# A sum of reciprocals on one core: a new work list with paired rows, multiply-and-accumulate sums and statistics put together by POOL

## The chip, the cores and the metric

The kernel runs on one core of a Trainium2 chip. The metric is the device time of an execution in microseconds, as the median of several executions; three runs of the kernel before are at hand. The profile shows one further execution, whose span is measured from its first to its last instruction.

## What is computed

The input x holds 32 x 512 x 1024 positive float32 numbers. The output is, for each of the 32 x 512 rows, the sum of the reciprocals of its 1024 numbers:

```python
def reference(x: np.ndarray) -> np.ndarray:
    return np.sum(1.0 / x, axis=-1).astype(np.float32)
```

That is 67.11 MB to read and 65,536 bytes to write.

## The kernel before, in words

The 16,384 rows lie on 128 partitions, 128 rows on each. What the kernel calls "row r" (0 to 127) is one row of 1024 numbers on every partition, 512 KB of data. A tile `ring` holds 48 rows; row r lives in place r modulo 48, so a load can start when the row 48 earlier is done. Row 127 comes as two units of 512 numbers (units 127 and 128), all others are one unit each.

No engine divides. ACT computes the reciprocal square root of a row in place (A, L150; one instruction may cover several rows), and each row's squares are then summed in one of four ways:

- B: DVE takes bn_stats of both half rows (L181) into `stats`: count, mean and variance of even and odd elements. K (L209 to L219) later turns the statistics of a group of columns into sums, as mean squared times 256 plus the variance term, adds the four parts and adds the result into `sums`. Rows that are not of kind B have zeros in `stats`, and rows of kind B zeros in `sums`, so K runs over whole stretches of columns.
- G and T: POOL squares rows in place (L191), DVE reduces them (TENSOR_REDUCE, L197).
- Z: ACT squares the row with an accumulator output (L161), which is two instructions, the second reading the accumulator.
- Q: DVE multiplies the row with itself and accumulates (tensor_tensor_reduce, L167).

The order of the work is written out by hand in `PLAN`, a list of words. A letter names the operation, the number its first unit, `+n` how many rows it takes. `D n` loads the next n rows (L141), as one DMA, or as two where the ring wraps. `O` stores the first 118 columns of `sums` in six pieces (L132). Every engine takes its own words in the order of the list: ACT takes A and Z; DVE takes B, Q, T and K; POOL takes G; SP issues D, O and the final store. Between engines, semaphores order reads and writes of the same place in a tile. The loads and stores use eight semaphores in turn, so an issue also waits until the transfer eight issues earlier has landed.

After the list, L228 adds the two parts of the last row's sum, and the last columns are stored.

Of the kernel before, what the change touches and what calls it, by code (L numbers as in the profile page):

```python
# [7 lines left out]


@with_exitstack  # L10
def kernel(
# [5 lines left out]
    nc = tc.nc  # L17
    f32 = mybir.dt.float32
    P = 128
    D = 1024  # L20
    H = D // 2
    F = 128
    R = 48
    PIECES = (512, 512)
    DONE = 118

    PLAN = """
        D16 D14 D13 A0+4 A4+4 B0 Q1 B2 A8+4 G4+3 B3 A12+4 B8 Q9 B10 Z7 G12+3 T4+3 D10 Z15 A16+4
        B11 A20+4 B16 T12+3 D9 A24+4 G20+3 B17 B18 B19 A28+2 B24 Z23 B25 G28+2 T20+3 D9 A30+4
        B26 B27 A34+4 T28+2 B30 A38+4 B31 D9 B32 B33 A42 B34 Z37 B35 A43+4 K0+32 B36 D5 B38
        A47+4 G44+2 B39 B40 B41 Z43 B42 D6 A51+2 T44+2 Z49 B46 D4 A53+4 B47 B48 B50 D4 A57+4 B51
        B52 B54 Z53 G59 B55 D5 A61 Z60 B56 G61 B57 A62+4 B58 D3 T59 D2 T61 A66+4 G63 K32+32 B64
        B65 Z62 G69 T63 D3 A70 B66 D3 G70 B67 B68 D2 A71+4 T69 T70 D2 A75+4 B71 B72 D2 B73 D1
        A79 G75 B74 D1 A80+4 B76 B78 T75 D1 D1 Z77 D1 D1 B79 D1 D1 A84 B80 A85+4 B81 B83 B84 Z82
        B85 A89+2 B86 A91+4 B87 B88 B89 A95+4 B90 B91 B92 Z96 B93 Z97 B94 A99+4 B95 B98 K64+32
        A103 B99 A104+3 G103 B101 B102 Z100 T103 G106 A107+2 B104 B105 A109+3 G107 T106 B108  # L40
        Z110 G109 T107 A112+3 B111 T109 A115+2 B112 B113 Z116 B114 A117+2 B115 A119+2 B117
        K96+22 O0 A121 G119 B120 A122 B121 Z118 B122 A123 T119 A124 B123 A125 G124 A126 B125
        A127 A128 K118+10 G127 T124 Z126 Z128 T127
    """.split()

    Arsqrt = mybir.ActivationFunctionType.Abs_reciprocal_sqrt
    Square = mybir.ActivationFunctionType.Square
    mult = mybir.AluOpType.mult
    add = mybir.AluOpType.add
# [7 lines left out]
            name=nc.get_next_instruction_name(),  # L57
# [4 lines left out]
    )  # L62

    pool = ctx.enter_context(tc.tile_pool(name="pool", bufs=1))
    ring = pool.tile([P, R, D], f32)
    stats = pool.tile([P, F, 2, 2, 3], f32)
    part = pool.tile([P, F, 4], f32)
    total = pool.tile([P, F], f32)
    sums = pool.tile([P, F + 1], f32)
    nc.gpsimd.memset(stats, 0.0)  # L70
    nc.gpsimd.memset(sums, 0.0)  # L71

    def parse(tok):
        r, _, n = tok[1:].partition("+")
        return tok[0], int(r), int(n or 1)

    def place(u):
        k = u - (F - 1)
        if k < 0:
            return u, 0, D  # L80
        return F - 1, sum(PIECES[:k]), PIECES[k]

    def area(u, n=1):
        r, at, w = place(u)
        return ring[:, r % R : r % R + n, at : at + w]

# [35 lines left out]
    def rows(u, n=1):  # L122
        spaces = []
        for r, at, w in (place(i) for i in range(u, u + n)):
            spaces += [("row", r % R, i) for i in range(at, at + w, 128)]
        return spaces

    loaded = 0
    left = set(range(DONE))

    def store(lo, hi):
        nc.sync.dma_start(out=out_v[:, lo:hi], in_=sums[:, lo:hi])  # L132

    with tc.manual_schedule():
        for op, u, n in (parse(tok) for tok in PLAN):
            if op == "D":
                n, u = u, loaded
                while n:
                    r, at, w = place(u)
                    m = min(n, R - r % R, F - 1 - u) if u < F - 1 else 1  # L140
                    inst = nc.sync.dma_start(  # L141
                        out=area(u, m), in_=x_v[:, r : r + m, at : at + w]
                    )
                    note("SP", inst, writes=rows(u, m))
                    u, n = u + m, n - m
                loaded = u
            elif op == "A":
                while n:
                    m = min(n, R - place(u)[0] % R)
                    inst = nc.scalar.activation(  # L150
                        out=area(u, m),
                        in_=area(u, m),
                        func=Arsqrt,
                        scale=1.0 - 2.0**-17,
                    )
                    note("ACT", inst, writes=rows(u, m))
                    u, n = u + m, n - m
            elif op == "Z":
                c = u - (F - 1) if u >= F else 0
                c = F if c else u  # L160
                inst = nc.scalar.activation(  # L161
                    out=area(u), in_=area(u), func=Square, accum_out=sums[:, c : c + 1]
                )
                note("ACT", inst, writes=rows(u))
            elif op == "Q":
                row = area(u)
                inst = nc.vector.tensor_tensor_reduce(  # L167
                    out=row,
                    in0=row,
                    in1=row,  # L170
                    scale=1.0,
                    scalar=0.0,
                    op0=mult,
                    op1=add,
                    accum_out=sums[:, u : u + 1],
                )
                note("DVE", inst, writes=rows(u))
            elif op == "B":
                r, at, w = place(u)
                for h in range(0, w, H):  # L180
                    inst = nc.vector.bn_stats(  # L181
                        out=stats[:, r, (at + h) // H],
                        in_=ring[:, r % R, at + h : at + min(h + H, w)],
                    )
                    half = [("row", r % R, i) for i in range(at + h, at + min(h + H, w), 128)]
                    note("DVE", inst, reads=half)
            elif op == "G":
                while n:
                    m = min(n, R - u % R)
                    row = area(u, m)  # L190
                    inst = nc.gpsimd.tensor_tensor(out=row, in0=row, in1=row, op=mult)  # L191
                    note("POOL", inst, writes=rows(u, m))
                    u, n = u + m, n - m
            elif op == "T":
                while n:
                    m = min(n, R - u % R)
                    inst = nc.vector.tensor_reduce(  # L197
                        out=sums[:, u : u + m],
                        in_=area(u, m),
                        axis=mybir.AxisListType.X,  # L200
                        op=add,
                    )
                    note("DVE", inst, reads=rows(u, m))
                    u, n = u + m, n - m
            elif op == "K":
                mean = stats[:, u : u + n, :, :, 1].rearrange("p f h e -> p (f h e)")
                var = stats[:, u : u + n, :, :, 2].rearrange("p f h e -> p (f h e)")
                tmp = part[:, u : u + n].rearrange("p f q -> p (f q)")
                nc.vector.tensor_tensor(out=tmp, in0=mean, in1=mean, op=mult)  # L209
                nc.vector.scalar_tensor_tensor(  # L210
                    out=tmp, in0=tmp, scalar=float(H // 2), in1=var, op0=mult, op1=add
                )
                nc.vector.tensor_reduce(  # L213
                    out=total[:, u : u + n],
                    in_=part[:, u : u + n],
                    axis=mybir.AxisListType.X,
                    op=add,
                )
                nc.vector.tensor_tensor(  # L219
                    out=sums[:, u : u + n],  # L220
                    in0=sums[:, u : u + n],
                    in1=total[:, u : u + n],
                    op=add,
                )
            elif op == "O":
                for c in range(0, DONE, DONE // 6):
                    store(c, min(c + DONE // 6, DONE))
        nc.vector.tensor_tensor(  # L228
            out=sums[:, F - 1 : F],
            in0=sums[:, F - 1 : F],  # L230
            in1=sums[:, F : F + 1],
            op=add,
        )
        store(DONE, F)


# [28 lines left out]
```

## Time and profile before

| what | us |
|---|---|
| median of 3 runs (172.34 to 172.53) | 172.5 |
| the profiled execution's own time | 171.93 |
| its span | 169.82 |
| DVE busy, ACT busy, POOL busy | 136.2, 135.8, 48.7 |
| first A on ACT starts | 23.10 |
| first bn_stats on DVE starts | 26.83 |
| last instruction that writes `sums` (L228) ends | 167.36 |

The profiled execution took 2.1 us more than its span, for what lies around the first and the last instruction. In the profile, "idle before" is the time that an engine stood still ahead of an instruction, and "<-" names what ended it. DVE has no idle time of note from 43.67 us to its end; all its idle time in the waits view, 30.3 us, lies before that. POOL waits for ACT for 113.5 us in all. TensorE does nothing in this kernel. The DMA queue of the loads is busy for 93.2% of the span, measured over the 16 DMA engines.

### The profile page before, as it was taken

To read this page: it belongs to the slowest core of one execution; us is meant where nothing else is said; L and a number is where in the kernel's file an instruction comes from. 1 tells how busy PE (TensorE), PEld (TensorE's weight loads), DVE (VectorE), ACT (ScalarE), POOL (GpSimd) and SP (SyncE) were. 2 spreads that over 40 slices of the span, in tenths; PEclk is the share of its full clock that TensorE was granted. 3 is DMA by queue.
4 is the path that set the end of the run, shared out by engine and by line. 5 is a ranking of instruction groups with operands and counts; after the bars stand their busy time and mean duration, and the time that the engine had idled before them with its cause. 6 is when DMAs were issued, how large, how long until landed. Compare 5 with 4: busy or idle time off the path is not lost.

```text
span 169.8 us, 437 instructions
## 1 busy us (share of the span) xinstructions
DVE 136.2 (80%) x207; ACT 135.8 (80%) x88; POOL 48.7 (29%) x24
## 2 busy tenths in 40 slices
DVE  0000006499799999999999999999999999999993
ACT  3000059998995899999998959999999999899923
POOL 4000000859089200070052580400000177104420
DMA  6998999999998999999999999999999999999600
GB/s 247 494 401 355 479 432 432 432 432 401 439 452 376 434 439 440 443 425 434 452 434 443 417 394 437 428 423 400 450 437 408 429 423 413 419 410 410 213 0 1
DMA packets 5331, 67.20 MB, mean 396 GB/s; under 512 B 1616, under 2 KB 1616, under 8 KB 2768
## 3 DMA queue, kind: packets, MB, share of 16 engines
q1 hardware_dynamic: 5328, 67.18, 93.2%
q14 instruction: 3, 0.02, 0.0%
HBM read 67.11 MB, written 0.07 MB: 396 GB/s over the span
## 4 chain that ended last, share of the span: by engine, by line
DVE 72%; DMA 23%; ACT 2%; issue 1%; SPq 0%; DVEq 0%
DVE stats L181 53%; DMA ring<-in_x_dram 23%; DVE sums L197 15%; ACT ring L150 2%; DVE part L209 1%; DVE sums L219 1%; DVE part L210 1%; DVE total L213 1%; SPq L141 0%; DVE sums L228 0%; DVEq L228 0%; DVEq L197 0%; DVEq L219 0%
## 5 line engine op out<-in xcount | busy, mean ns | idle before, releaser
L150 ACT ACTIVATE ring<-ring 128x4096 f32<-128x4096 f32 (+4 forms) x49 | 115.8, 2419 | 27.2 <-DMA ring<-in_x_dram 27.0
L181 DVE BATCH_NORM_STATS2 stats<-ring 128x6 f32<-128x512 f32 x164 | 99.3, 680 | 30.3 <-ACT ring L150 30.3
L191 POOL TENSOR_TENSOR ring<-ring 128x1024 f32<-128x1024 f32 (+3 forms) x18 | 47.0, 2609 | 113.5 <-ACT ring L150 113.5
L197 DVE TENSOR_REDUCE sums<-ring 128x1 f32<-128x1024 f32 (+3 forms) x18 | 29.4, 1649 | 0.1
L161 ACT ACTIVATE ring<-ring 128x1024 f32<-128x1024 f32 (+1 forms) x19 | 19.4, 1021 | 3.2 <-DVE sums L219 3.2
L161 ACT ACTIVATION_READ_ACCUMULATOR ring<-ring 128x1 f32 x19 | 3.5, 186 | 0.0
L167 DVE CUSTOM_DVE_ANT_0 ring<-ring 128x1024 f32<-128x1024 f32 x2 | 2.9, 1466 | 0.0
L209 DVE TENSOR_TENSOR part<-stats 128x128 f32<-128x128 f32 (+2 forms) x5 | 2.5, 502 | 0.1
L219 DVE TENSOR_TENSOR sums<-sums,total 128x32 f32<-128x32 f32 (+2 forms) x5 | 2.2, 438 | 0.2
L55 ACT ACT_TABLE_LOAD x1 | 1.3, 1283 | 0.7 <-PEq L249 0.7
L210 DVE SCALAR_TENSOR_TENSOR part<-part,stats 128x128 f32<-128x128 f32 (+2 forms) x5 | 1.5, 300 | 0.2
L70 POOL MEMSET stats<- 128x1536 f32 x1 | 1.4, 1378 | 0.3 <-POOLq L249 0.3
L213 DVE TENSOR_REDUCE total<-part 128x32 f32<-128x128 f32 (+2 forms) x5 | 1.3, 260 | 0.2
L228 DVE TENSOR_TENSOR sums<-sums 128x1 f32<-128x1 f32 x1 | 0.2, 160 | 0.1
L71 POOL MEMSET sums<- 128x129 f32 x1 | 0.2, 208 | 0.0
L249 POOL MEMSET const-float32-0.0<- 128x1 f32 x1 | 0.1, 99 | 0.2 <-issue 0.2
L167 DVE DVE_READ_ACCUMULATOR2_ANT sums<- 128x1 f32 x2 | 0.2, 80 | 0.0
L249 POOL MEMSET const-bfloat16-1.0<- 128x1 bf16 x1 | 0.1, 103 | 0.0
L249 POOL MEMSET const-uint8-127<- 128x1 uint8 x1 | 0.1, 103 | 0.0
L249 POOL MEMSET const-float32-1.0<- 128x1 f32 x1 | 0.1, 99 | 0.0
## 6 DMA issues: line engine op xcount, KB each, us to landing
ring<-in_x_dram SPq DMA_DIRECT2D x3, 4608.0 KB, 32.6
ring<-in_x_dram SPq DMA_DIRECT2D x4, 2560.0 KB, 38.4
ring<-in_x_dram SPq DMA_DIRECT2D x1, 7168.0 KB, 38.8
ring<-in_x_dram SPq DMA_DIRECT2D x1, 6656.0 KB, 54.1
ring<-in_x_dram SPq DMA_DIRECT2D x4, 1536.0 KB, 36.5
ring<-in_x_dram SPq DMA_DIRECT2D x4, 1024.0 KB, 28.6
ring<-in_x_dram SPq DMA_DIRECT2D x7, 512.0 KB, 19.6
ring<-in_x_dram SPq DMA_DIRECT2D x1, 3072.0 KB, 36.9
```

The source lines that it names most:

```text
L55: nc.scalar.add_instruction(mybir.InstLoadActFuncSet(name=nc.get_next_instruction_name(), act_func_set_id=act_sets.index("abs_reciprocal_s ...
L70: nc.gpsimd.memset(stats, 0.0)
L150: inst = nc.scalar.activation(out=area(u, m), in_=area(u, m), func=Arsqrt, scale=1.0 - 2.0**-17,)
L161: inst = nc.scalar.activation(out=area(u), in_=area(u), func=Square, accum_out=sums[:, c : c + 1])
L167: inst = nc.vector.tensor_tensor_reduce(out=row, in0=row, in1=row, scale=1.0, scalar=0.0, op0=mult, op1=add, accum_out=sums[:, u : u + 1],)
L181: inst = nc.vector.bn_stats(out=stats[:, r, (at + h) // H], in_=ring[:, r % R, at + h : at + min(h + H, w)],)
L191: inst = nc.gpsimd.tensor_tensor(out=row, in0=row, in1=row, op=mult)
L197: inst = nc.vector.tensor_reduce(out=sums[:, u : u + m], in_=area(u, m), axis=mybir.AxisListType.X, op=add,)
L209: nc.vector.tensor_tensor(out=tmp, in0=mean, in1=mean, op=mult)
L210: nc.vector.scalar_tensor_tensor(out=tmp, in0=tmp, scalar=float(H // 2), in1=var, op0=mult, op1=add)
L213: nc.vector.tensor_reduce(out=total[:, u : u + n], in_=part[:, u : u + n], axis=mybir.AxisListType.X, op=add,)
L219: nc.vector.tensor_tensor(out=sums[:, u : u + n], in0=sums[:, u : u + n], in1=total[:, u : u + n], op=add,)
```

## The change

The list is new, and with it come new operations:

- The ring has 46 places. Row 127 comes as 640 and 384 numbers. The loads are 24 words instead of 27: D2 D9 D11 D11 D13, then D12 D10 D10 D7 D7 D7 D6 D5 D4 D3 D2 D2 D1 D2 and five D1.
- Ten rows (32, 43, 47, 61, 100, 104, 105, 108, 111, 114) are summed as pairs, by 1/a + 1/b = (a + b) / (a b), where a is the first half of the row and b the second. POOL multiplies the halves into a slot of `prod` (P), TensorE adds them into a PSUM bank by two matmuls with an identity matrix (U), ACT takes the reciprocal square root of the product, scaled, and squares it (L and E, 512 numbers each), and DVE multiplies the result with the sums in PSUM and accumulates (R, a tensor_tensor_reduce).
- There are 35 Q (two of them the pieces of row 127, the second of which starts from the first one's sum), 23 B, 36 rows of G, 20 Z, and 41 rows of T. Five T rows are squared by ACT without an accumulator (C).
- K appears twice, for columns 0 to 63 and 64 to 115, and runs on POOL as five instructions; it no longer touches `sums`. A new word M, also on POOL, adds all of these columns into `sums` at once, ahead of the store O of columns 0 to 115. Columns 116 to 127 hold no B row.
- L228 is gone.
- At the start POOL makes the identity matrix (a memset and an affine_select on 128 x 128) ahead of the memsets of `stats` and `sums`.

The diff, cut to its core:

```diff
-    R = 48
-    PIECES = (512, 512)
-    DONE = 118
+    R = 46
+    NP = 5
+    PIECES = (640, 384)
+    NR = F - sum(PIECES) // D
+    KB = (0, 64, 116)
+    S = float(2**17)
+    FIT = 1.0 - 2.0**-17
...
+        D2 D9 D11 D11 D13 A0+2 Z0 Z1 A2 A3+5 A8 Q6 G3 A9+2 Q7 C8 T3 C9 Z2 Z4 Z5 A11 A12 G10+2
+        A13 A14+7 G12+2 T8+6 D12 A21 G16+3 Z19 Z20 Z21 A22+7 U32@0 P32@0 B14 Q15 T16+2 T18 D10
...
+        Q83 Z81 G80 A85+4 T79 D1 G84 T80 D1 D1 D1 T84 A89 B85 A90+2 Q86 Z82 Q87 Z88 Q89 A92+2
+        B90 Q91 A94 B92 A95+2 Q94 A97+2 Q95 Q96 Z93 G97 U100@4 B98 A99 A101 P100@4 T97 A102 B99
+        P104@0 L100 U104@5 A103 B101 G102 L104 B103 E100 E104 R100 A106+2 P105@1 U105@6 T102
+        P108@2 R104 U108@7 L105 B106 A109 L108 Q107 K64+52 E105 E108 R105 A110 U111@0 R108 Q109
+        P111@3 A112+2 Q110 L111 Q112 E111 U114@1 P114@4 A115 R111 Q113 A116 L114 Q115 A117+2
+        Q116 E114 Q117 A119+2 R114 M0 O0 Q118 A121 Q120 Z119 Q121 A122 A123 Q122 A124 Q123 A125
+        Q124 A126 Q125 A127 A128 Q127 Z126 Q128
...
+            elif op == "P":
+                slot[u], r = b, u % R
+                inst = nc.gpsimd.tensor_tensor(
+                    out=prod[:, b], in0=ring[:, r, :H], in1=ring[:, r, H:], op=mult
+                )
...
+            elif op == "U":
+                bank[u], r = b, u % R
+                for h in range(2):
+                    inst = nc.tensor.matmul(
+                        ps[:, b],
+                        lhsT=ident,
+                        rhs=ring[:, r, h * H : (h + 1) * H],
+                        start=h == 0,
+                        stop=h == 1,
+                    )
...
+            elif op in "LE":
+                pair = prod[:, slot[u]]
                 inst = nc.scalar.activation(
+                    out=pair,
+                    in_=pair,
+                    func=Arsqrt if op == "L" else Square,
+                    scale=S * FIT if op == "L" else 1.0,
+                )
...
+            elif op == "R":
+                pair = prod[:, slot[u]]
+                inst = nc.vector.tensor_tensor_reduce(
+                    out=pair,
+                    in0=pair,
+                    in1=ps[:, bank[u]],
+                    scale=S,
+                    scalar=0.0,
+                    op0=mult,
+                    op1=add,
+                    accum_out=sums[:, u : u + 1],
+                )
...
             elif op == "K":
...
+                nc.gpsimd.tensor_tensor(out=flat, in0=mean, in1=mean, op=mult)
+                nc.gpsimd.tensor_scalar(
+                    out=flat, in0=flat, scalar1=float(H // 2), scalar2=None, op0=mult
+                )
+                nc.gpsimd.tensor_tensor(out=flat, in0=flat, in1=var, op=add)
+                nc.gpsimd.tensor_tensor(
+                    out=part[:, u : u + n, :2],
+                    in0=part[:, u : u + n, :2],
+                    in1=part[:, u : u + n, 2:],
                     op=add,
                 )
+                nc.gpsimd.tensor_tensor(
+                    out=total_b[:, u : u + n],
+                    in0=part[:, u : u + n, 0],
+                    in1=part[:, u : u + n, 1],
                     op=add,
                 )
+            elif op == "M":
+                nc.gpsimd.tensor_tensor(
+                    out=sums[:, : KB[-1]],
+                    in0=sums[:, : KB[-1]],
+                    in1=total_b[:, : KB[-1]],
+                    op=add,
+                )
...
-        nc.vector.tensor_tensor(
-            out=sums[:, F - 1 : F],
-            in0=sums[:, F - 1 : F],
-            in1=sums[:, F : F + 1],
-            op=add,
-        )
-        store(DONE, F)
+        store(KB[-1], F)
```

More of the change, by code (lines that the diff above doesn't have):

```diff
@@ L7 @@
 from concourse.hw_specs import get_activation_tables
+from concourse.masks import make_identity
 @with_exitstack
@@ L22 @@
     F = 128
-    R = 48
-    PIECES = (512, 512)
-    DONE = 118
-    PLAN = """
[L32 to L43, printed above, removed]
+    R = 46
@@ new lines @@
+    NP = 5
[4 more added lines that the diff above has]
+    FIT = 1.0 - 2.0**-17
+    PLAN = """
+        D2 D9 D11 D11 D13 A0+2 Z0 Z1 A2 A3+5 A8 Q6 G3 A9+2 Q7 C8 T3 C9 Z2 Z4 Z5 A11 A12 G10+2
+        A13 A14+7 G12+2 T8+6 D12 A21 G16+3 Z19 Z20 Z21 A22+7 U32@0 P32@0 B14 Q15 T16+2 T18 D10
+        A29 G24 A30+2 Q22 G25+3 L32 Q23 Z30 E32 T24 Z31 R32 G28+2 A33 U43@1 A34+4 P43@1 T25+5
+        D10 A38 G34+2 A39 A40 Q37 A41+2 G36 Q38 L43 A44+2 G40+2 B39 T34+3 E43 C33 Z42 G44+2 A46
+        U47@2 T33 D7 A48+2 T40+2 A50+2 G46 R43 T44+2 D7 A52 P47@2 A53 G48 T46 L47 A54+2 B49 G51
+        T48 A56 Q54 A57 G52 E47 Z50 B55 G53 U61@3 A58+3 R47 B56 P61@3 T51+3 D7 A62+3 G58 B57 L61
+        G62+3 A65 T58 D6 A66 B59 A67 E61 B65 C60 R61 C67 T60 K0+64 Z66 T62+3 D5 A68+4 T67 D4 A72
+        Q68 A73+5 B69 Q70 D3 B71 B72 D2 A78+6 G74 B75 B76 T74 B77 A84 G79 B78 Z73 D2 D1 D2 D1
+        Q83 Z81 G80 A85+4 T79 D1 G84 T80 D1 D1 D1 T84 A89 B85 A90+2 Q86 Z82 Q87 Z88 Q89 A92+2
[5 more added lines that the diff above has]
+        Q124 A126 Q125 A127 A128 Q127 Z126 Q128
@@ L64 @@
     pool = ctx.enter_context(tc.tile_pool(name="pool", bufs=1))
+    pspool = ctx.enter_context(
+        tc.tile_pool(name="pspool", bufs=1, space=bass.MemoryType.PSUM)
+    )
     ring = pool.tile([P, R, D], f32)
@@ L67 @@
     part = pool.tile([P, F, 4], f32)
-    total = pool.tile([P, F], f32)
-    sums = pool.tile([P, F + 1], f32)
+    total_b = pool.tile([P, F], f32)
+    sums = pool.tile([P, F], f32)
+    prod = pool.tile([P, NP, H], f32)
+    ident = pool.tile([P, P], f32)
+    ps = pspool.tile([P, 8, H], f32)
+    make_identity(nc, ident)
     nc.gpsimd.memset(stats, 0.0)
@@ L73, in parse @@
     def parse(tok):
-        r, _, n = tok[1:].partition("+")
-        return tok[0], int(r), int(n or 1)
+        body, _, b = tok[1:].partition("@")
+        r, _, n = body.partition("+")
+        return tok[0], int(r), int(n or 1), int(b or 0)
     def place(u):
-        k = u - (F - 1)
-        if k < 0:
+        if u < NR:
             return u, 0, D
-        return F - 1, sum(PIECES[:k]), PIECES[k]
+        at = sum(PIECES[: u - NR])
+        return NR + at // D, at % D, PIECES[u - NR]
     def area(u, n=1):
@@ L126, in rows, with half @@
         return spaces
+    def half(u, at):
+        return [("row", u % R, i) for i in range(at, at + H, 128)]
     loaded = 0
-    left = set(range(DONE))
+    summed = set()
+    slot, bank = {}, {}
     def store(lo, hi):
@@ L134 @@
     with tc.manual_schedule():
-        for op, u, n in (parse(tok) for tok in PLAN):
+        for op, u, n, b in (parse(tok) for tok in PLAN):
             if op == "D":
@@ L139 @@
                     r, at, w = place(u)
-                    m = min(n, R - r % R, F - 1 - u) if u < F - 1 else 1
+                    m = min(n, R - r % R, NR - u) if u < NR else 1
                     inst = nc.sync.dma_start(
@@ L146 @@
                 loaded = u
[L147 to L154, printed above, removed]
-                    )
-                    note("ACT", inst, writes=rows(u, m))
-                    u, n = u + m, n - m
+            elif op in "AC":
+                inst = nc.scalar.activation(
+                    out=area(u, n),
+                    in_=area(u, n),
+                    func=Arsqrt if op == "A" else Square,
+                    scale=FIT if op == "A" else 1.0,
+                )
+                note("ACT", inst, writes=rows(u, n))
@@ L158 @@
             elif op == "Z":
-                c = u - (F - 1) if u >= F else 0
-                c = F if c else u
                 inst = nc.scalar.activation(
-                    out=area(u), in_=area(u), func=Square, accum_out=sums[:, c : c + 1]
+                    out=area(u), in_=area(u), func=Square, accum_out=sums[:, u : u + 1]
                 )
                 note("ACT", inst, writes=rows(u))
+            elif op == "P":
[3 more added lines that the diff above has]
+                )
+                note("POOL", inst, rows(u), [("slot", b)])
+            elif op == "U":
[8 more added lines that the diff above has]
+                    )
+                    note("PE", inst, half(u, h * H), [("bank", b)])
+            elif op in "LE":
+                pair = prod[:, slot[u]]
+                inst = nc.scalar.activation(
+                    out=pair,
[3 more added lines that the diff above has]
+                )
+                note("ACT", inst, writes=[("slot", slot[u])])
+            elif op == "R":
[10 more added lines that the diff above has]
+                )
+                note("DVE", inst, [("bank", bank[u])], [("slot", slot[u])])
@@ L165 @@
             elif op == "Q":
-                row = area(u)
+                row, r = area(u), place(u)[0]
+                total = sums[:, r : r + 1]
                 inst = nc.vector.tensor_tensor_reduce(
@@ L171 @@
                     scale=1.0,
-                    scalar=0.0,
+                    scalar=total if r in summed else 0.0,
                     op0=mult,
                     op1=add,
-                    accum_out=sums[:, u : u + 1],
+                    accum_out=total,
                 )
+                summed.add(r)
                 note("DVE", inst, writes=rows(u))
             elif op == "B":
-                r, at, w = place(u)
-                for h in range(0, w, H):
+                for h in range(2):
                     inst = nc.vector.bn_stats(
-                        out=stats[:, r, (at + h) // H],
-                        in_=ring[:, r % R, at + h : at + min(h + H, w)],
-                    )
-                    half = [("row", r % R, i) for i in range(at + h, at + min(h + H, w), 128)]
-                    note("DVE", inst, reads=half)
+                        out=stats[:, u, h], in_=ring[:, u % R, h * H : (h + 1) * H]
+                    )
+                    note("DVE", inst, reads=half(u, h * H))
             elif op == "G":
[L188 to L193, printed above, removed]
-            elif op == "T":
[L195 to L200, printed above, removed]
-                        op=add,
-                    )
-                    note("DVE", inst, reads=rows(u, m))
-                    u, n = u + m, n - m
+                row = area(u, n)
+                inst = nc.gpsimd.tensor_tensor(out=row, in0=row, in1=row, op=mult)
+                note("POOL", inst, writes=rows(u, n))
+            elif op == "T":
+                inst = nc.vector.tensor_reduce(
+                    out=sums[:, u : u + n],
+                    in_=area(u, n),
+                    axis=mybir.AxisListType.X,
+                    op=add,
+                )
+                note("DVE", inst, reads=rows(u, n))
             elif op == "K":
@@ L207 @@
                 var = stats[:, u : u + n, :, :, 2].rearrange("p f h e -> p (f h e)")
[L208 to L211, printed above, removed]
-                )
[L213 to L216, printed above, removed]
+                flat = part[:, u : u + n].rearrange("p f q -> p (f q)")
+                nc.gpsimd.tensor_tensor(out=flat, in0=mean, in1=mean, op=mult)
+                nc.gpsimd.tensor_scalar(
+                    out=flat, in0=flat, scalar1=float(H // 2), scalar2=None, op0=mult
+                )
+                nc.gpsimd.tensor_tensor(out=flat, in0=flat, in1=var, op=add)
[3 more added lines that the diff above has]
+                    in1=part[:, u : u + n, 2:],
                     op=add,
                 )
[L219 to L222, printed above, removed]
+                nc.gpsimd.tensor_tensor(
+                    out=total_b[:, u : u + n],
+                    in0=part[:, u : u + n, 0],
+                    in1=part[:, u : u + n, 1],
+                    op=add,
+                )
+            elif op == "M":
[3 more added lines that the diff above has]
+                    in1=total_b[:, : KB[-1]],
                     op=add,
@@ L225 @@
             elif op == "O":
-                for c in range(0, DONE, DONE // 6):
-                    store(c, min(c + DONE // 6, DONE))
-        nc.vector.tensor_tensor(
-            out=sums[:, F - 1 : F],
-            in0=sums[:, F - 1 : F],
-            in1=sums[:, F : F + 1],
-            op=add,
-        )
-        store(DONE, F)
+                for c in range(0, KB[-1], 20):
+                    store(c, min(c + 20, KB[-1]))
+        store(KB[-1], F)
 _INS = ['x']
```

## The prediction

> **What bounds the kernel now.** I read the page first (engine totals and the chain that ended last), then the waits, then the timeline of the first 60 us and of the last 15.
>
> ```profile
> span 169.8 us, 437 instructions
> ...
> DVE 136.2 (80%) x207; ACT 135.8 (80%) x88; POOL 48.7 (29%) x24
> ...
> DVE 72%; DMA 23%; ACT 2%; issue 1%; SPq 0%; DVEq 0%
> ```
> ```profile
> DVE stats L181 <- ACT ring L150: 30.3, 3, 26.8
> ACT ring L150 <- DMA ring<-in_x_dram: 27.0, 6, 21.1
> ```
>
> Two engines are busy for 80% each, and the chain is DVE for 72% of the span: no engine is short of hours, but DVE begins late and then never stops. ACT waits 21.1 us for the 16 rows of the first transfer, DVE 26.8 us for ACT's first group.
>
> ```profile
> 23.10 14.14 ACT L150 ACTIVATE ring<-ring 128x4096 f32<-128x4096 f32 x4 [21.08 <-DMA ring<-in_x_dram]
> ...
> 40.02 12.43 ACT L150 ACTIVATE ring<-ring 128x4096 f32<-128x4096 f32 x4 [0.71 <-DMA ring<-in_x_dram]
> ...
> 55.76 11.58 ACT L150 ACTIVATE ring<-ring 128x4096 f32<-128x4096 f32 x4 [2.27 <-DMA ring<-in_x_dram]
> ```
>
> These three waits end when the first (16 rows), second (14) and third (13) transfer land. 16.9 / 14 and 15.7 / 13 both give 1.21 us a row; 23.1 - 16 x 1.21 = 3.7, so the first n rows are there at 3.7 + 1.21 n. All 128 could be there at 158.6. The issues of L141 say when they are:
>
> ```profile
> L141 SPq DMA_DIRECT2D ring<-in_x_dram x29: 327/328/945, 0.7 to 152.4; - x29
> ...
> DMA to landing us min/median/max: 9.0/30.9/59.7
> ```
>
> The last of 29 loads is issued at 152.4 and takes at least 9.0: it lands at about 161.4, 2.8 later than the bare rate. But work goes on until 167.4:
>
> ```profile
> 164.29 0.21 DVE L209 TENSOR_TENSOR part<-stats 128x40 f32<-128x40 f32 x1
> ...
> 165.28 1.06 ACT L161 ACTIVATE ring<-ring 128x1024 f32<-128x1024 f32 x1 [3.15 <-DVE sums L219]
> ...
> 167.20 0.16 DVE L228 TENSOR_TENSOR sums<-sums 128x1 f32<-128x1 f32 x1
> ```
>
> So DVE is 6 us behind the data, and even ACT's Z126 waits 3.15 for it, because the last K adds into the same columns of sums. After 167.36 come 2.46 us of store and end (span 169.82).
>
> **DVE's work after.** From the timeline, start to start: bn_stats 0.594 a half row, TENSOR_REDUCE 1.07 a row + 0.05, multiply-and-accumulate (Q, L167) 28.03 to 29.16 = 1.13 a row. The new list has 23 B rows (27.3), 41 T rows in 23 instructions (45.0), 33 full Q rows and two pieces (37.3 + 1.2), ten R, each taken as half a Q plus its accumulator read, 0.6 (6.0): 116.8 against 136.2. The five K (7.5 us: 2.5 + 1.5 + 1.3 + 2.2) and L228 leave DVE altogether.
>
> **ACT's work after.** Four 4-row A take 14.14, and a 1-row A is followed 0.95 later (87.32 to 88.27): 0.853 a row + 0.10 an instruction. 118 rows in 65 instructions are 107.2; 20 Z at 1.04 (37.15 to 38.19) 20.8; five C at 0.95 4.8; 20 L and E on 512 elements at 0.52 (the 0.61 row less the overlap) 10.4. Sum 143.2, against 133.4 for the old list by the same rows. ACT becomes the fuller engine.
>
> **Start.** Two rows land at 6.2, A0+2, Z0 and Z1 take 3.9 (to 10.1), then ACT idles to 17.0, when rows 2 to 10 are there. From there 139.3 us of ACT work fit before 160. Up to row 109 I count nothing for ACT and DVE but the wait for data. Identity and both memsets run on POOL ahead of Z0 at 8.1; the old memsets end at 2.26, identity's two instructions are between 0.2 (L71, 129 elements) and 2 x 1.04 (L191 with 512 elements): covered by 5.8 us, and by 6.9 more of ACT's idling. Ring rows: 46 instead of 48 means that each load waits for rows 2 earlier; rows 46 to 57 need T8+6, which the sums above put near 45, while the loads already queued last until 59.4. A cover of about 14 us; gone, each microsecond past it delays all later rows by one.
>
> **POOL's work after.** L191 is 1.71 a row + 0.18: 36 G rows in 24 instructions 65.9, ten P 10.4 (512 elements, 1.04). K64 is five instructions on 208, 208, 208, 104 and 52 elements, 0.54 + 0.35 + 0.54 + 0.36 + 0.28 = 2.1 by L191's slope (bounds: five times 0.2 and five times 1.04); K0 2.3. With M and the start about 84, against 48.7. POOL is half idle, so only its place matters: K64 stands ahead of P111 and P114, on which L111, L114 wait.
>
> **The tail, which sets the end.** The new list has 24 loads; five fewer of 29 take the 2.8 us of excess to 2.3: last landing 160.9. Three paths then end together.
> - Data: A128 (0.43), Z126 (1.04 + its read 0.19): 162.6.
> - ACT: rows 110 to 113 land near 142.5 (3.7 + 114 x 1.21 = 141.6, with half the excess). From A110 on: 15 rows in 12 instructions 14.0, two pieces 1.1, Z119 and Z126 2.1, four L and E 2.1, 19.3 in all: 161.8.
> - DVE: from 143.5 (A110 done), 14 Q rows 15.8, pieces 1.2, R111 and R114 1.2: 161.7; Q128 after A128 ends at 161.9.
>
> So the last write of sums is at 162.6, and I add 0.5 for handoffs between engines (0.1 from A's end to POOL or DVE at the starts, some five in a row): 163.1. The K of the end, Z126's wait and L228 are gone: M on POOL covers columns below 116 only, and its store's six issues go out before. The final store waits for no load still under way. 163.1 + 2.46 = **165.6 span**. The profiled execution took 171.93 for a span of 169.82; 165.6 + 2.1 = 167.7, and the median of the runs is 0.57 above that execution: **168.3**.
>
> **The shared port.** Two-input DVE instructions stretch while POOL runs:
>
> ```profile
> 135.01 1.95 POOL L191 TENSOR_TENSOR ring<-ring 128x1024 f32<-128x1024 f32 x1 [24.92 <-ACT ring L150]
> ```
> ```profile
> 135.56 1.45 DVE L219 TENSOR_TENSOR sums<-sums,total 128x32 f32<-128x32 f32 x1
> ```
>
> L219 takes 0.19 elsewhere; here it ends at 137.01, just behind POOL's 136.96. The Q at 34.97 (1.72 against 1.21) and L209 at 94.78 (1.09) end just behind POOL too, while bn_stats and TENSOR_REDUCE keep their times. The list now has 35 Q instead of 2, and no row shows POOL starting during a Q. The Trainium skill (SBUF — State Buffer, Who interferes with whom) says that whichever starts first holds the port for its whole instruction and the other blocks, for DVE instructions with two SBUF inputs against POOL instructions that read SBUF. By that rule each P or K instruction could also lose up to one Q, 1.13, and R, whose second input is in PSUM, nothing.
>
> **Rivals.**
> 1. Waits on POOL in the tail. Half of 35 Q meeting POOL and waiting 1.3 on average would be 22 us; DVE has 143 us (19 to 162) for 117 of work, so 26 to spare, and until row 109 it costs little. Behind that K64, P111, P114 and M (4.5 together) stand among back-to-back Q, and ACT has 0.8 to spare for L111 and L114. Half of the 4.5, 2.3 to 2.4, lost: 170.7. The same holds if K64 costs its upper bound (5.2 - 2.1 - 0.8 = 2.3). For it: the three rows. Against: the order leaves POOL free behind P114, where eleven Q stand.
> 2. Slower: TensorE. No row of before has a matmul. Between nothing and twice the slowest row on 512 elements (2 x 1.04 = 2.1); I take 1.04, the row itself. Single pairs up to row 61 have over 10 us between landing and R. But rows 99 to 104 land near 131.5, and from there twelve matmuls (100, 104, 105, 108, 111, 114) come in one line. R108 needs eight of them; behind it DVE has 18.8 us of work (14 Q, pieces, three R), so it must start at 143.1 for 161.9. That holds up to 1.45 us a matmul; each 0.1 above costs 0.8. The median of before is passed from 2.0; at 2.2 it is 131.5 + 17.6 - 143.1 = 6.0 late: 174.3. The Trainium skill (FP8 and Floating Point Precision, TensorE Precision Notes) gives a true fp32 product four passes, and TensorE: Matmul & The Clock Gate (Part 1) 427 ns for 512 columns cold and 216 warm. By these an estimate is 1.7 us cold and 0.86 warm, that is 2.0 us late (170.3) if the array stays cold and nothing if it warms in the line.
> 3. Loads end early: were the excess of 2.8 all due to the small loads of the end, it might fall by 2 more: with ACT and DVE at 161.8 only 0.8 comes of it, unless those sums are high too; 166.4.
> 4. The list does less than it says: DVE still the bound. 116.8 + 3.5 + 26.8 would not reach 150, so only through rival 1; no more than 0.02 is left for no difference.
>
> **How the numbers follow.** Forecast 168.3, own range 166.8 to 169.8: 0.62. Rival 1: 0.19 (169.8 to 172). Rival 2 past 172.8: 0.11. Rival 3: 0.06. No difference: 0.02. The range 166.2 to 171.6 leaves out rival 2, a little of 1 and half of 3. A measurement can tell about 0.2%. Faster 0.62 + 0.18 + 0.06 = 0.86, same 0.02, slower 0.12 (a hundredth from rival 1).
>
> **What would show it.** After: ACT's first A near 6.2, 7 us of idling ahead of the second transfer, the last load landed near 161, DVE near 117 busy, ACT near 145, the last write of sums within 2.5 of the last landing. Q far above 1.21 or POOL instructions above L191's times mean the port. Wrong if R waits for PE in the last 35 us, if ACT waits for POOL over 1 us there, or if SP waits on ring rows so long that the loads run dry.

## The result, and the profile after

The changed kernel takes 178.16 us (median of four runs, 177.93 to 178.27) against 172.42 us for the kernel before on the same chip: a ratio of 1.0334, with a 95% interval of 1.0316 to 1.0352. It is slower by 5.7 us, where 168.3 us was forecast. The profiled execution took 177.93 us, with a span of 175.8.

The page of the changed kernel, engine totals and the chain that ended last:

```profile
span 175.8 us, 543 instructions
...
PE 27.6 (16%) x40; PEld 9.6 (5%) x40; DVE 135.6 (77%) x159; ACT 145.4 (83%) x131; POOL 99.2 (56%) x53
...
ACT 42%; DMA 23%; POOL 20%; DVE 8%; another core or an unknown queue 2%; issue 2%; SPq 1%; DVEq 0%
```

DVE is busy for 135.6 us, almost what it was (136.2), though the list leaves it 116.8 us of work by the rows of before. POOL has 99.2 where 84 were counted. The chain, which was DVE with some DMA, now passes through ACT, POOL and DVE.

The beginning is as forecast (timeline of ACT; start, duration, and in brackets the idle time before):

```profile
5.46 1.91 ACT L170 ACTIVATE ring<-ring 128x2048 f32<-128x2048 f32 x1 [3.46 <-DMA ring<-in_x_dram]
...
16.34 10.05 ACT L170 ACTIVATE ring<-ring 128x1024 f32<-128x1024 f32 x6 [6.69 <-DMA ring<-in_x_dram]
```

The end is not. The loads are done by 160 us (no data moves from 160 to 165), and yet work goes on for 13 us. The timeline of the last 30 us shows why:

```profile
148.21 1.45 POOL L258 TENSOR_TENSOR part<-stats 128x208 f32<-128x208 f32 x1 [5.29 <-DVE stats L238]
...
153.53 1.14 POOL L269 TENSOR_TENSOR total_b<-part 128x52 f32<-128x52 f32 x1
154.63 2.48 POOL L184 TENSOR_TENSOR prod<-ring 128x512 f32<-128x512 f32 x2
155.92 1.29 ACT L201 ACTIVATE prod<-prod 128x512 f32<-128x512 f32 x2 [8.31 <-POOL prod L184]
...
172.44 0.62 DVE L224 CUSTOM_DVE_ANT_0 ring<-ring,sums 128x384 f32<-128x384 f32 x1
```

Read from the bottom: the last multiply-and-accumulate ends at 173.06. ACT stood still for 8.31 us until POOL had multiplied the pair of row 111 (P111, L184). POOL could not do that earlier, since K64 (L258 to L269) stands ahead of it in POOL's queue, and K64 waited 5.29 us for DVE's statistics of row 106. Then it took 6.5 us (148.21 to 154.67) instead of the 2.1 of the prediction. So DVE was late by row 106, though it stood still only at the start, ahead of T8+6 and T25+5 (which starts at 61.97), and behind K64. Its waits, all of them (total, times, longest):

```profile
DVE ring L224 <- ACT ring L170: 21.9, 1, 21.9
DVE sums L247 <- POOL ring L244: 12.6, 2, 10.9
DVE prod L210 <- ACT prod L201: 2.7, 1, 2.7
```

What made it late stands in the durations, not in the waits (groups of instructions, shapes apart; busy us, mean ns):

```profile
L224 DVE CUSTOM_DVE_ANT_0 ring<-ring 128x1024 f32<-128x1024 f32 x33 | 56.4, 1743 | 22.0 <-ACT ring L170 21.9
...
L244 POOL TENSOR_TENSOR ring<-ring 128x1024 f32<-128x1024 f32 x15 | 31.3, 2102 | 41.8 <-ACT ring L170 41.7
```

A Q takes 1.74 us on average instead of 1.21: 33 x 0.53 = 17.6 us, nearly all that DVE is busy beyond the 116.8. A 1-row G takes 2.10 instead of 1.89. If the shared port is the cause, wait and work are one number in these rows; the experiments test it.

### The profile page after: what moved, and what is told of

The parts are those of the page before. It is cut to its first block, busy times and chain, and to the rows that moved or that the text cites. A ratio compares the mean times of both kernels' runs of the same rounds, so it can differ in the third digit from the quotient of the medians.

```text
span 175.8 us, 543 instructions
## 1 busy us (share of the span) xinstructions
PE 27.6 (16%) x40; PEld 9.6 (5%) x40; DVE 135.6 (77%) x159; ACT 145.4 (83%) x131; POOL 99.2 (56%) x53
## 4 chain that ended last, share of the span: by engine, by line
ACT 42%; DMA 23%; POOL 20%; DVE 8%; another core or an unknown queue 2%; issue 2%; SPq 1%; DVEq 0%
ACT ring L170 34%; DMA ring<-in_x_dram 23%; POOL ring L244 12%; DVE ring L224 5%; ACT ring L178 5%; POOL prod L184 5%; ACT prod L201 3%; DVE stats L238 1%; DVE prod L210 1%; POOL part L262 1%; POOL part L258 1%; POOL part L263 1%; SPq L163 1%; POOL total_b L269 1%
## 5 line engine op out<-in xcount | busy, mean ns | idle before, releaser
L170 ACT ACTIVATE ring<-ring 128x1024 f32<-128x1024 f32 (+6 forms) x70 | 113.8, 1687 | 15.3 <-DMA ring<-in_x_dram 15.3
L244 POOL TENSOR_TENSOR ring<-ring 128x1024 f32<-128x1024 f32 (+2 forms) x24 | 72.5, 3040 | 49.9 <-ACT ring L170 49.8
L224 DVE CUSTOM_DVE_ANT_0 ring<-ring 128x1024 f32<-128x1024 f32 (+1 forms) x34 | 57.1, 1716 | 22.0 <-ACT ring L170 21.9
L247 DVE TENSOR_REDUCE sums<-ring 128x1 f32<-128x1024 f32 (+4 forms) x23 | 46.3, 2040 | 12.6 <-POOL ring L244 12.6
L191 PE MATMUL ps<-ring,ident 128*128 128x512 f32 x40 | 27.6, 837 | 120.3 <-DMA ring<-in_x_dram 120.3
L238 DVE BATCH_NORM_STATS2 stats<-ring 128x6 f32<-128x512 f32 x46 | 28.7, 675 | 0.0
L201 ACT ACTIVATE prod<-prod 128x512 f32<-128x512 f32 x20 | 12.0, 618 | 11.0 <-POOL prod L184 11.0
L178 ACT ACTIVATE ring<-ring 128x1024 f32<-128x1024 f32 x20 | 20.8, 1041 | 0.1
L191 PEld LDWEIGHTS ps<-ring,ident 128*128 128x128 f32 x40 | 9.6, 261 | 137.4 <-DMA ring<-in_x_dram 85.3
L184 POOL TENSOR_TENSOR prod<-ring 128x512 f32<-128x512 f32 x10 | 14.5, 1462 | 0.0
L258 POOL TENSOR_TENSOR part<-stats 128x256 f32<-128x256 f32 (+1 forms) x2 | 2.1, 1042 | 8.1 <-DVE stats L238 8.1
L269 POOL TENSOR_TENSOR total_b<-part 128x64 f32<-128x64 f32 (+1 forms) x2 | 1.4, 720 | 0.2
```

The lines of the kernel that those rows point to most:

```text
L170: inst = nc.scalar.activation(out=area(u, n), in_=area(u, n), func=Arsqrt if op == "A" else Square, scale=FIT if op == "A" else 1.0,)
L178: inst = nc.scalar.activation(out=area(u), in_=area(u), func=Square, accum_out=sums[:, u : u + 1])
L184: inst = nc.gpsimd.tensor_tensor(out=prod[:, b], in0=ring[:, r, :H], in1=ring[:, r, H:], op=mult)
L191: inst = nc.tensor.matmul(ps[:, b], lhsT=ident, rhs=ring[:, r, h * H : (h + 1) * H], start=h == 0, stop=h == 1,)
L201: inst = nc.scalar.activation(out=pair, in_=pair, func=Arsqrt if op == "L" else Square, scale=S * FIT if op == "L" else 1.0,)
L224: inst = nc.vector.tensor_tensor_reduce(out=row, in0=row, in1=row, scale=1.0, scalar=total if r in summed else 0.0, op0=mult, op1=add, acc ...
```

## The experiments

Two theories stood at the start. **A**: Q and POOL hold each other up at the port, DVE has no time to spare for it, and K64's place passes the delay on. **B**: the place of K64 alone does it.

The kernel before was run again beside each group of four experiments, with medians of 172.12, 171.95 and 171.98 us, against 172.42 beside the changed kernel. So a difference between two kernels of different groups is good to about half a microsecond; each ratio is to the kernel before of its own group.

**K64 behind the pairs.** One word moves.

```diff
-        ... B106 A109 L108 Q107 K64+52 E105 E108 ... E114 Q117 A119+2 R114 M0 O0 ...
+        ... B106 A109 L108 Q107 E105 E108 ... E114 Q117 A119+2 R114 K64+52 M0 O0 ...
```

> The changed list with one word moved: K64+52 (the POOL statistics of columns 64 to 115) stands behind all pairs, just ahead of M, instead of ahead of P111 and P114. Theory A (the shared port: in the changed kernel 33 full Q took 1.74 us each instead of 1.21, so DVE is some 6 us late by row 106, and K64's place passes that on to ACT, which waits 8.3 us for P111): ACT's wait at L111 goes, but DVE stays late. From B106's end (148.1) DVE still has 15 Q, two pieces and four R, 20.9 us, so the last write of sums stays near 169 to 171, and the time is 174 to 176. Theory B (the place of K64 alone; DVE's lateness is covered): the end follows the last load, and the time is 168 to 170.

Measured: 175.31 us, ratio to before 1.019 (1.0175 to 1.0205). The waits of ACT for POOL at L201 fall from 11.0 to 3.1 us in all, the longest from 8.3 to 1.1. DVE stays late and ends at 170.2. The place of K64 is worth 2.9 us as long as DVE is late; theory B, which expected 168 to 170, falls.

**The Q of rows below 106 as B.** Eighteen words change their letter: Q6, Q7, Q15, Q22, Q23, Q37, Q38, Q54, Q68, Q70, Q83, Q86, Q87, Q89, Q91, Q94, Q95, Q96.

```diff
-        ... A8 Q6 G3 A9+2 Q7 ... Q94 A97+2 Q95 Q96 Z93 G97 ...
+        ... A8 B6 G3 A9+2 B7 ... B94 A97+2 B95 B96 Z93 G97 ...
```

> The changed list with the 18 Q of rows below 106 turned into B in the same places (two bn_stats of one SBUF input each, 1.19 us, instead of one multiply-and-accumulate with two, 1.13), K64 where it was. Theory A: no wait at the port before row 106, so DVE is some 12 us lighter and no longer late, POOL's instructions take L191's times of before again, K64 starts near 142 instead of 148.2, ACT's wait at L111 falls from 8.3 to under 2, and the time is 167 to 170. Theory B: Q's waits at the port were spare time of DVE, K64 still starts near 147 and the time stays at 176 to 178.

Measured: 170.62 us, ratio 0.9919 (0.9903 to 0.9936): 7.5 us less than the changed kernel, with the same rows and slightly dearer DVE instructions. Its groups show that both sides get their times back, and its timeline that K64 starts 7.3 us earlier:

```profile
L244 POOL TENSOR_TENSOR ring<-ring 128x1024 f32<-128x1024 f32 x15 | 28.2, 1892 | 47.3 <-ACT ring L170 47.3
...
L224 DVE CUSTOM_DVE_ANT_0 ring<-ring 128x1024 f32<-128x1024 f32 x15 | 18.5, 1286 | 0.1
```
```profile
140.95 1.45 POOL L258 TENSOR_TENSOR part<-stats 128x208 f32<-128x208 f32 x1 [0.97 <-DVE stats L238]
...
148.68 1.29 ACT L201 ACTIVATE prod<-prod 128x512 f32<-128x512 f32 x2 [3.51 <-POOL prod L184]
```

ACT still waits 3.51 us for P111, since K64 is as long as before (it stands among Q107 to Q112, which stayed), so the time is a little above the 167 to 170 that theory A expected; theory B expected 176 to 178.

**The pairs undone.** The words P, U, L, E and R of the ten pair rows go; L becomes A and R becomes B, and K64 stands ahead of M.

```diff
-        ... U111@0 R108 Q109 P111@3 A112+2 Q110 L111 Q112 E111 U114@1 P114@4 A115 R111 ...
+        ... B108 Q109 A112+2 Q110 A111 Q112 A115 B111 ...
```

> The changed list with the ten pair rows taken as A and B (no P, U, L, E, R), K64 just ahead of M since row 114 is then a B row. ACT then waits for no other engine. Theory A: DVE gains ten B of 1.19 for ten R of 0.61, 5.8 us more, less about 3 of port waits at P; it is late all the same and sets the end: 175 to 178. Theory B (ACT's stall behind POOL is the cause): 168 to 170.

Measured: 179.89 us, ratio 1.0455 (1.0438 to 1.0472). This is 1.9 us above the 175 to 178 of theory A, and far from the 168 to 170 of theory B. ACT waits for nothing but data, and the kernel is slower still: the chain is DVE for 60%, and DVE's last Q ends at 175.0. Against the list with K64 late (175.31) the ten pairs save 4.6 us, where the expectation had about 3 net. They are no fault of the change.

**The early start alone.** The kernel before, with its first loads cut smaller.

```diff
-        D16 D14 D13 A0+4 A4+4 B0 Q1 B2 ...
+        D4 D8 D8 D10 D13 A0+4 A4+4 B0 Q1 B2 ...
```

> The kernel before with only its first three loads cut otherwise (4, 8, 8, 10 and 13 rows instead of 16, 14 and 13). The early start alone: ACT's first A at 8.5 instead of 23.1, DVE some 14 us earlier. DVE has 136 us of work and was 6 us behind the last load, so if the start is worth what the prediction took it for, the end moves by 3 to 5 us and the time is 167.5 to 169.5. If the early rows only mean waiting later (rows 20 to 42 land when they did), the time stays within 1 us of 172.5.

Measured: 170.50 us, ratio 0.9908 (0.9893 to 0.9923): 1.6 us, between the two expectations. From its page and its waits:

```profile
DMA 63%; ACT 23%; DVE 8%; another core or an unknown queue 3%; SPq 1%; issue 0%; DVEq 0%
```
```profile
DVE stats L181 <- ACT ring L150: 27.3, 5, 11.9
```

DVE waits almost as long as before (27.3 against 30.3 us), only in five pieces: it starts at 11.9 and then has to wait for the rows of later loads. The chain is DMA for 63% of the span, and DVE from 152.2 us on: this list follows the data, and its last write of `sums` (to 166.4) comes some 5 us behind the last load.

**Both edits.** The eighteen Q as B, and K64 behind the pairs (the two diffs above together).

> The changed list with both edits: the 18 Q of rows below 106 as B, and K64 behind the pairs. If the time of the changed kernel is the port before row 106 plus K64's place, ACT's remaining wait of 3.5 us at L111 and DVE's 2.7 at R111 go, and the last write of sums comes 2 to 3.5 earlier than with the Q turned into B alone: 167 to 168.6. If K64's place only mattered while DVE was late, nothing is left to gain: 170 to 171.

Measured: 168.67 us, ratio 0.9812 (0.9798 to 0.9827), at the upper end of the 167 to 168.6 expected. ACT waits for no other engine any more. ACT's last instruction and DVE's, and the group of the 15 full Q that are left:

```profile
161.24 0.19 ACT L178 ACTIVATION_READ_ACCUMULATOR ring<-ring 128x1 f32 x1
...
163.11 0.62 DVE L224 CUSTOM_DVE_ANT_0 ring<-ring,sums 128x384 f32<-128x384 f32 x1
```
```profile
L224 DVE CUSTOM_DVE_ANT_0 ring<-ring 128x1024 f32<-128x1024 f32 x15 | 19.5, 1350 | 0.0
```

DVE ends at 163.73, where the prediction had put the last write at 163.1. So without the eighteen Q and with K64 behind the pairs the time is near the forecast, but that it comes so near is in part luck. ACT and the data are done at 161.43, 1.2 us before the 162.6 of the forecast's data path. DVE, which the forecast had done at 161.9, ends 1.8 later: its 15 full Q still take 0.14 more than 1.21 each, 2.1 us in all, all of it on six Q beside P111, P114, K64 and M. That is about the 2.3 that rival 1 had as the price of the tail.

**No Q below row 116.** As both edits, and Q107, Q109, Q110, Q112, Q113 and Q115 as B too.

> As the list with both edits, and rows 107 to 115 are B too, so that no Q runs below row 116. K64 then starts behind B115 and meets Q116 and later. If the port costs something only where a Q meets POOL, this moves the same few meetings (K64 beside Q) later: within 1 us of the list with both edits. If the Q between 107 and 115 also slow P111 and P114, 1 to 2 us faster.

Measured: 168.41 us, ratio 0.9791 (0.9772 to 0.9809), the lowest median here; its interval overlaps that of both edits, so a gain is not shown. As expected, little is left in those six.

**DVE's idle time at the start.** T8+6 split, in the changed list.

```diff
-        ... Q7 C8 T3 C9 Z2 Z4 Z5 A11 A12 G10+2 A13 A14+7 G12+2 T8+6 D12 ...
+        ... Q7 C8 T3 C9 T8+2 Z2 Z4 Z5 A11 A12 G10+2 A13 A14+7 G12+2 T10+4 D12 ...
```

> The changed list with T8+6, on which DVE waits 10.9 us for POOL (it starts at 38.0), split: T8+2 right behind C9, T10+4 where T8+6 was. DVE then does 2.2 us of work in that idle time. If DVE has no time to spare before row 106 (theory A), K64 starts some 2 us earlier and the time falls by 1 to 2.5: 175.7 to 177.2. If the idle time of the start is spare, nothing changes: 178.

Measured: 177.96 us, ratio 1.0352 (1.0337 to 1.0368), no difference from the changed kernel. In this form theory A was wrong: DVE does run 2 us earlier at row 14, but T25+5 waits for POOL and starts at 62.1 as before. What DVE gains up to there is given back there. The same split on top of both edits gave nothing either:

> All three edits. Without the port DVE has spare time, so the split of T8+6 should do nothing here (theory A): within 0.7 us of the list with both edits. If it helps by more than 1 us, DVE is still the bound in the first half.

Measured: 168.88 us, ratio 0.982 (0.9804 to 0.9837), as theory A expected.

**Which Q cost the time.** Three kernels turn a few Q into B, all else as in the changed list: Q37 and Q38; Q6, Q7, Q15, Q22 and Q23; Q94, Q95 and Q96.

```diff
-        D10 A38 G34+2 A39 A40 Q37 A41+2 G36 Q38 L43 A44+2 G40+2 B39 ...
+        D10 A38 G34+2 A39 A40 B37 A41+2 G36 B38 L43 A44+2 G40+2 B39 ...
```

> The changed list with two words changed: Q37 and Q38 into B. In the changed kernel these two took 2.54 and 4.61 us beside POOL's G36 and G40+2, and from then on DVE has no gap until row 106. Theory A, refined (a port wait counts only where DVE has no later gap to make it up in): DVE is 4.6 us earlier from T33 to B106, K64 starts near 143.6, and the time falls by 4 to 5: 173.2 to 174.2. Rival (all port waits count alike, in proportion to their length): these are 4.7 of 17.5 us of waits, so 4.7 / 17.5 of the 7.5 that all 18 gave, 2.0: 176.2.

Measured: 172.96 us, ratio 1.0055 (1.0036 to 1.0075). Two letters give 5.2 us (K64 starts 4.9 earlier), a little more than the 4 to 5 of the refined theory and far more than a proportional share of 2.0.

> The changed list with Q6, Q7, Q15, Q22 and Q23 into B. They hold the longest wait (Q23 took 6.31 us), 7.7 us in all. Theory A, refined: behind them DVE waits for POOL at T25+5, which moves by 1.6 only (61.98 to 60.37 where all were B), so 1 to 1.8 of gain: 176.4 to 177.2. Rival (in proportion): 7.7 / 17.5 of 7.5, 3.3: 174.9.

Measured: 174.12 us, ratio 1.0119 (1.0095 to 1.0144), 4.0 us: more than either theory. T25+5 does move by 1.7 only. Most of the rest comes from what follows, Q37 and Q38, which were left alone. In the changed kernel (DVE, then POOL):

```profile
67.38 2.54 DVE L224 CUSTOM_DVE_ANT_0 ring<-ring 128x1024 f32<-128x1024 f32 x1
...
69.85 4.61 DVE L224 CUSTOM_DVE_ANT_0 ring<-ring 128x1024 f32<-128x1024 f32 x1
```
```profile
63.39 16.38 POOL L244 TENSOR_TENSOR ring<-ring 128x2048 f32<-128x2048 f32 x5 [0.22 <-ACT ring L170]
```

and with the five Q turned, DVE:

```profile
65.64 2.85 DVE L224 CUSTOM_DVE_ANT_0 ring<-ring 128x1024 f32<-128x1024 f32 x1
...
68.42 2.90 DVE L224 CUSTOM_DVE_ANT_0 ring<-ring 128x1024 f32<-128x1024 f32 x1
```

POOL has G34+2, G36 and G40+2 in a row here. When both engines have only such work, they take turns, one instruction each. In the changed kernel Q37 fell in the turn behind the 1-row G36 and Q38 behind the 2-row G40+2; arriving 1.7 us earlier, they fell behind G34+2 (already half done) and G36, and cost 1.4 us less (2.85 + 2.90 against 2.54 + 4.61). With 1.7 that is 3.1 of the 3.7 by which K64 starts earlier; the rest is the balance of the later Q, some dearer and some cheaper, for they meet other POOL instructions too. What a Q costs is what is left of the POOL instruction in front of it, so a shift of the order changes all later costs.

> The changed list with Q94, Q95 and Q96 into B. They took 1.71, 2.28 and 2.27 beside G97, P100 and P104, 2.6 us of waits on DVE, and POOL's three took 6.9 instead of 4.4. Both theories expect 2.6 less of DVE's delay less the 0.2 that three B cost more; by the refined theory all of it counts, since no gap follows: 175.4 to 176.2. In proportion it would be 1.1: 177.0.

Measured: 175.73 us, ratio 1.0217 (1.0196 to 1.0238), as the refined theory expected.

Over all kernels that keep K64's place, the time follows K64's start (from each one's timeline):

| kernel | K64 starts | time | difference |
|---|---|---|---|
| the change | 148.21 | 178.16 | 29.95 |
| T8+6 split | 148.24 | 177.96 | 29.72 |
| Q94 to Q96 as B | 146.17 | 175.73 | 29.56 |
| Q6 to Q23 as B | 144.52 | 174.12 | 29.60 |
| Q37, Q38 as B | 143.32 | 172.96 | 29.64 |
| all 18 as B | 140.95 | 170.62 | 29.67 |

The times are medians; with the profiled executions' own times the difference is 29.6 to 29.8 in all six. K64 waits for B106, so its start is DVE's progress at row 106. Behind it nothing makes up a microsecond.

**The early start on the new list.** Both edits, but the first loads large again.

```diff
-        D2 D9 D11 D11 D13 A0+2 Z0 Z1 ...
+        D16 D14 D16 A0+2 Z0 Z1 ...
```

> The list with both edits (18 Q as B, K64 late), but with first loads of 16, 14 and 16 rows instead of 2, 9, 11, 11 and 13, which undoes the early start alone. ACT has 143 us of work and would begin at 23.1: 143 + 23.1 less nothing gives an end of at least 166.3 and the time at least 171; with ACT's later waits 172 to 175. If the early start is worth as little as with the old list (1.6 us), 169.5 to 171.

Measured: 176.12 us, ratio 1.0238 (1.0218 to 1.0258), 7.5 us more than with the small first loads; the forecast was 172 to 175. One wait on ACT tells it:

```profile
ACT ring L170 <- DMA ring<-in_x_dram: 21.0, 1, 21.0
```

ACT is busy for 144.4 us in this kernel, 1.3 of it a table load before the first row, and begins on the rows at 22.97, so it cannot end before 166.1; it ends at 168.98, against 161.43 with the small loads. In the old list ACT is busy for 136.1, and with small first loads it still waits 26.6 us for data, so that an earlier start buys little there.

## Why the prediction was wrong, point by point

- **The start: right.** First A at 5.46 (6.2 forecast), then 6.7 us of idling (6.9). **What bounds the kernel before: right in part.** DVE begins late and then never stops, as was said, but the late start alone costs little: with the first A at 8.21 the old list gains 1.6 us, because its engines then wait for later data.
- **ACT's work: right.** 145.4 busy, against 135.8 for the old list, which the same rows gave as 143.2 and 133.4.
- **The last load: 1.3 us earlier than forecast.** Forecast 160.9; the last of the 24 loads is issued at 148.3 and lands 11.3 us later, at 159.6. That is what rival 3 described, and it changed nothing, since the data did not set the end.
- **TensorE (rival 2): did not come true.** The two matmuls of a pair took 3.78 us at 58.77 and at 85.97, at a granted clock of 0.50, and 1.99 at 142.18 and at 145.86, at 1.00; four in a line took 3.70 from 137.29, at 1.00. No R waited for PE, neither here nor in the list with both edits, where DVE is on time. The Trainium skill (FP8 and Floating Point Precision, TensorE Precision Notes, with TensorE: Matmul & The Clock Gate, Part 1) was the source of the prediction's estimates, 1.7 us a matmul cold and 0.86 warm. The trace is near both, with 1.89 at a clock of 0.50 and 0.93 in the line at 1.00; but the first pair, at 43.12, took 3.42 although the profile gives the clock as 1.00 there.
- **The port (rival 1): the right mechanism, mis-sized, and given 0.19.** Its sum of waits was near, 22 us estimated and 17.6 measured, though not spread as assumed (half of the Q at 1.3 us each): ten Q below row 106 hold 16.7 of it, Q23 alone 5.1 and Q38 3.4. The step that failed is "26 to spare, and until row 109 it costs little", by which the forecast put these waits at nothing. DVE's first instruction came at 21.9, not 19, which leaves 140 us to 161.9. T8+6 and T25+5 wait 12.6 us for POOL, which the sum left out. 140 - 12.6 - 116.8 leaves 10.6 us, not 26, and 17.6 do not fit: DVE was 7.3 us late at row 106 (K64 at 148.21 instead of the 140.95 with the eighteen Q as B). That 17.6 - 10.6 comes near 7.3 is no proof of the size, since it counts gaps and waits wherever they lie. The 7.7 us of waits ahead of T25+5 moved it by only 1.6 (61.97 against 60.37), while the 9.0 behind it found no gap up to K64.
- **A reading of the prediction was wrong.** It says that the Q at 34.97 ends just behind POOL. POOL's instruction ends at 35.61 (30.30 + 5.31) and the Q at 36.69, 1.08 behind: the Q waits for POOL's end and then does nearly all its work. The price of 1.72 for that Q was read rightly.
- **What the lateness does: missed.** The rival priced the tail's waits at 2.4 us. K64 was put at 2.1 us; undisturbed, K0 takes 3.3 (100.55 to 103.87), and among Q, K64 takes 6.5. Late start and length together made ACT wait 8.31 us for P111, with all its remaining rows queued behind; the prediction had named a wait of ACT for POOL of over 1 us as a sign of being wrong. The runs split the 9.9 us between forecast and result: 7.5 for the Q below row 106, 2.0 more for K64's place once they are gone, and 0.4 is left (168.67 against 168.3), each good to about half a microsecond; the 0.4 also hides the two errors of the tail that cancel, told above. The two rows of K0 (POOL):

```profile
100.55 0.64 POOL L258 TENSOR_TENSOR part<-stats 128x256 f32<-128x256 f32 x1 [2.82 <-DVE stats L238]
...
103.57 0.30 POOL L269 TENSOR_TENSOR total_b<-part 128x64 f32<-128x64 f32 x1
```

- **The rule at the port holds in both directions.** P beside Q takes 2.25 us (133.18 to 137.63 for two) and alone 1.27, so POOL waits for DVE as DVE waits for POOL. The Trainium skill (SBUF — State Buffer, SBUF: two separate sides) says of a DVE instruction with two SBUF inputs and a GpSimd instruction that reads SBUF that the one that starts first has the port for its whole length, and the other blocks. The trace agrees. R, whose second input is in PSUM, falls outside that rule, and the trace agrees here too: its mean is 675 ns, and it takes 0.67 at 59.54, beside a POOL instruction of 57.36 to 61.94. R writes to SBUF like Q, so the write is not what makes Q wait.
- **The chances.** Rival 1 was held to cost at most 172, because its price was worked out at the tail alone. A delay that starts in the middle had no rival of its own. Slower had 0.12, nearly all of it for TensorE, which had no part in it.

## What to carry to other kernels

In these profiles a wait at the shared port is counted as busy time (a Q has 1.74 us instead of 1.21), so compare the mean duration of each shape with the same shape undisturbed before trusting an engine's busy share. Spare time is only spare up to the next place where two engines meet: subtract every wait on another engine first, and ask at which later instruction a delay can still be made up. An instruction that is needed late (here K64) should not stand in an in-order queue ahead of one that another engine needs now.

## What the runs showed of the hardware that was not expected

- DVE and POOL take turns at the port, instruction by instruction, where both have only such work, so a DVE Q of 1.21 us lost from nothing to 5.1 us, by the size of POOL's instruction. In the changed kernel, Q22 and Q23 on DVE, then G24 and G25+3 on POOL:

```profile
50.11 2.13 DVE L224 CUSTOM_DVE_ANT_0 ring<-ring 128x1024 f32<-128x1024 f32 x1
...
52.17 6.31 DVE L224 CUSTOM_DVE_ANT_0 ring<-ring 128x1024 f32<-128x1024 f32 x1
```
```profile
49.26 1.89 POOL L244 TENSOR_TENSOR ring<-ring 128x1024 f32<-128x1024 f32 x1 [3.97 <-ACT ring L170]
...
51.11 6.29 POOL L244 TENSOR_TENSOR ring<-ring 128x3072 f32<-128x3072 f32 x1
```

Q22 ends 1.09 behind G24's end (51.15), G25+3 (5.31 undisturbed) ends at 57.40, 5.16 behind Q22's end, and Q23 1.08 behind that.

- POOL's product of two different halves takes 1.27 us for 512 elements, where a square of 512 took 1.04. Small POOL instructions were dearer than the forecast's 2.3 us: five of K0, on 256 to 64 elements, take 3.3 us with the gaps.
- Four of K64's five instructions lost most of a Q each where Q stood on DVE: 52 elements took 1.14 us there, and 64 elements 0.30 without a Q beside them. The fifth (208 elements, 0.73 us, at 149.74) stood beside two R and lost nothing.
